# Two transformer blocks on one core: some transfers go to ScalarE's queue, the merges' operands become 66 wide, the order is planned anew

## Chip, cores, metric

One core of a Trainium2 chip. The metric is the device time of one execution in microseconds; the time before is the median of three runs.

## What is computed

Two blocks in a row on 256 tokens of width 1024, fp32 in and out. The first has block attention and differential attention with a table of relative biases, attention to a memory of 256 rows, and a gated feed-forward layer of 2816; the second an RWKV-7 layer with 12 heads of 64, memory attention and feed-forward, then a latent-attention layer with the same. What the change touches:

```python
logits = logits + bias_ht[h_i[..., None], rel_bucket(dist)]     # first block: biases by distance

def step(state, inp):                                           # second block: RWKV-7 scan over tokens
    r_t, w_t, k_t, v_t, a_t, b_t = inp
    sa = jnp.einsum('bhvk,bhk->bhv', state, a_t)
    state = (state * w_t[:, :, None, :] + sa[..., None] * b_t[:, :, None, :]
             + v_t[..., None] * k_t[:, :, None, :])
    return state, jnp.einsum('bhvk,bhk->bhv', state, r_t)
```

## The kernel before

**Matrix products.** Each fp32 product is three TensorE (PE) products of halves: a panel of weights (`wr`, 128 x 1024 numbers, 512 KB, three buffers) comes in by SP's queue, is cast to its high half `wh` on ScalarE (ACT) or VectorE (DVE), and DVE subtracts to get `wl`; activations are held as `ah` and `al`. The products gather in PSUM tiles `acc`; all other PSUM tiles are `pst`.

**The order.** The program is written as tasks (coroutines) whose operations are recorded first. The class `Order` then plans them: a list scheduler with a cost for each operation, a latency from engine to engine, times for DMA queues (`DMA_ISSUE`, `DMA_START`), a price for changing between widths of stationary operands (`turn`), and tables: `RUSH` moves the due times of a kind of task, `LEAN` and `SIDE` set what runs on which of two engines. What comes out is one fixed list for each engine, DMA issues included, since an issue stands in the queue of the engine that makes it. Each engine runs its list in order and waits where it must. The planner's costs decide the list, nothing at run time does. All recorded instructions are issued from one line, 2730 in the profile of before.

**Start.** `first_norm` loads the tokens `x` (`xres`) in four pieces; `load_gains` loads all gains; both stand in SP's queue between panels of `w_in`. ACT loads its function table, casts panels, and makes `ah` from x and gains.

**Bias table.** `rel_bias` makes a vector of biases (`relvec`) with three small matmuls, writes it to DRAM (`relonce`), writes it out 24 times (`rel`), and reads it back as the table `bias` in two transfers of 768 KB. DVE adds `bias` to the scores (`e`), ACT takes exponentials, and TensorE transposes them.

**The inverses.** The scan is done in two chunks of 128 tokens for 12 heads, 24 units, each with a unit triangular matrix of 128 x 128 to invert (`inverses`). `products` multiplies `bt` by `ar`, masks into `m271` (first chunk, halves `l` and `h`) and `m272` (second), and writes to DRAM (`d_m`). `substitute` reads the 32 x 32 blocks on the diagonal into rows (`kk` for the first chunk, a `tm` stage for the second) and substitutes in 31 steps of two instructions, the first chunk on POOL, the second on DVE; it writes the result to `d_x`. In `rwkv`, `expand` reads `d_x` into `xt` and DVE multiplies by a mask; `grams` makes the masked products `mk`, `mr` of two heads at a time; `merge` joins the blocks to 64 and to 128 for four units at a time, six times. Its matmuls have as stationary operands the inverse `xt`, the masked matrix (`mb(u)`) and zero-padded copies `y4`, `y2` in `ymerge`; 144 instructions of these are 64 columns wide:

```python
nc.tensor.matmul(p[:64, 1, i], y4[:, i], pairs(xt[:, u]), start=True, stop=True)
nc.tensor.matmul(p[:, i], self.mb(u)[:, 64:], x[:, i, :64], start=True, stop=True)
nc.tensor.matmul(p[:, i], y2[:, i], xt[:, u, 64:], start=True, stop=True)
```

Of the kernel before, what the change touches and what calls it, by code (L numbers as in the profile page):

```python
# [266 lines left out]
class Order:  # L267
# [22 lines left out]
    DMA_ISSUE = {"sync": 450.0, "gpsimd": 1000.0}  # L290
    DMA_START = {"sync": 1100.0, "gpsimd": 1900.0}
# [124 lines left out]
    def play(self, succs, preds, level, back):  # L416
# [9 lines left out]
        order, dma, table = [], 0.0, None  # L426
# [62 lines left out]
        while len(order) < len(ops):  # L489
            if events:  # L490
                i = events.pop()
                finish(i, ready[i] if back else 0.0)
                continue
            at, e = min((free[e] if here[e] else max(free[e], coming[e][0][0]), e) for e in names if here[e] or coming[e])
            while coming[e] and coming[e][0][0] <= at + self.EPS:
                i = heapq.heappop(coming[e])[1]
                heapq.heappush(here[e], (-level[i], i))
            i = heapq.heappop(here[e])[1]
            if not opened(i, at):
                continue  # L500
            op, start = ops[i], max(ready[i], free[e])
            if op.what != "dma_start":
                cost = op.cost
                if op.port:
                    start = max(start, port["gpsimd" if e == "vector" else "vector"])
                elif e == "tensor" and not back:
                    start = max(ready[i], free[e] + self.turn(mode, op.mode))
                    mode = op.mode
                    if start > free[e] + self.COLD:
                        slow = start + self.WARM  # L510
                    if start > free[e] + 40.0 and start == ready[i]:
                        cost += self.FILL
                    if start < slow:
                        cost *= 1.8
                end = start + cost
                if op.tables and table not in op.tables:
                    table = op.tables[0]
                    end += self.TABLE
                free[e] = end
                if op.port:  # L520
                    port[e] = end + self.PORT
            elif back:
                dma = max(dma, ready[i]) + op.size / 360.0
                free[e] = end = max(free[e] + self.DMA_ISSUE[e], dma + self.DMA_START[e])
            else:
                free[e] = start + self.DMA_ISSUE[e]
                dma = end = max(dma, start + self.DMA_START[e]) + op.size / (360.0 if start > self.DMA_COLD else 240.0)
            finish(i, end)
# [57 lines left out]

LEAN = {'ab0': 2895, 'carry': 137, 'diff_heads': 125, 'expand1': -3988, 'ffn': 1004, 'w_out': -297, 'gate': 3000, 'small': 4209, 'grams1': 1044, 'a_w_out': 168, 'mix_qk': -3000, 'grams0': 161, 'solve1': 808, 'merge1': 1298, 'a_r384': 3000, 'ab1': 6275, 'room': 128, 'mem': 1690, 'w_in': 770, 'cross_kv_w': 61, 'cross': -65, 'expand0': 537, 'down_w': -84, 'norm1': -235, 'a_lora2304': -49, 'rope': 3462, 'first': -431, 'a_mem_out': 1112, 'b_mem_heads': -246, 'a_mem_kv': -519}

SIDE = {'last': 'vector', 'gate': 'vector', 'kk': 'vector', 'rope': 'vector', 'sq': 'vector', 'x': 'vector'}

# [144 lines left out]
class Net(Sched):  # L737
# [1390 lines left out]
    def inverses(self, filler):  # L2128
# [36 lines left out]
        def substitute(c):  # L2165
# [16 lines left out]
            for i in range(2):  # L2182
                nc.sync.dma_start(ms[48 * i:48 * i + 48], d_m[c].strided(0, [[32 * 128 + 32, 48], [128, 32], [1, 32]]))
# [603 lines left out]
```

## Time and profile before

| | |
|---|---|
| runs | 1138.84, 1139.57, 1144.20 us; median 1139.57 |
| profiled execution | 1143.02 us, span 1141.3, mean granted TensorE clock 0.986 |
| busy share of the span | PE 97%, weight loads 92%, DVE 75%, ACT 38%, POOL 15% |
| TensorE products of the panels (`acc`) | 73% of the chain that ended last |
| transfers | 183.27 MB, 161 GB/s on the mean |

The span is from the first to the last instruction of the profiled execution; times in the rows below are from its start. An engine's idle time is put down to what ended it.

### The profile page before, as it was taken

Reading aid. Unit: us, or ns where it says so; the run is one execution under the profiler, and the core shown is the slowest. Engines: PE = TensorE matmul, PEld = TensorE weight load, DVE = VectorE, ACT = ScalarE, POOL = GpSimd, SP = SyncE. Lnnn points to the kernel's source line nnn. Section 1 sums busy time; section 2 is a strip of 40 time slices with the busy share of each in tenths; the row PEclk is TensorE's granted clock in tenths of the full one; section 3 lists DMA queues with packets and bytes.
Section 4 is the critical chain, followed back from the end, with each engine's and each line's share of the span. In section 5 each row is a group of like instructions: output and inputs, shape, how many; then the busy total and the mean of one; then the engine's idle time right before and its main releaser. Section 6 shows DMA issues by size and latency. Waiting matters only on the chain.

```text
span 1141.3 us, 21650 instructions
## 1 busy us (share of the span) xinstructions
PE 1110.4 (97%) x8716; PEld 1052.6 (92%) x8716; DVE 854.8 (75%) x1454; ACT 429.5 (38%) x857; POOL 171.3 (15%) x199
## 2 busy tenths in 40 slices
PE   8899999999999999899979999999999999999997
PEld 7798999999999999799768999999999889999985
DVE  7658577677776777979787877766878968777584
ACT  5437442545223214635323532223235765212400
POOL 1200101024111013016601121120012002111100
PEclk9999999999999999899989999999999999999999
DMA  8744355266564655347320355556654425555563
GB/s 260 231 153 145 120 176 181 86 193 208 168 208 140 214 187 180 121 117 215 102 65 14 96 182 180 176 163 186 195 169 140 153 95 170 184 185 179 175 207 105
DMA packets 116164, 183.27 MB, mean 161 GB/s; under 512 B 19175, under 2 KB 41480, under 8 KB 116040
## 3 DMA queue, kind: packets, MB, share of 16 engines
q1 hardware_dynamic: 115920, 181.37, 51.8%
q8 instruction: 68, 1.11, 0.4%
q0 software_dynamic: 144, 0.52, 0.2%
q14 instruction: 32, 0.26, 0.1%
HBM read 178.84 MB, written 3.48 MB: 160 GB/s over the span
## 4 chain that ended last, share of the span: by engine, by line
PE 84%; DVE 8%; DMA 4%; ACT 2%; issue 1%; SPq 0%; POOLq 0%; POOL 0%; ACTq 0%; DVEq 0%
PE acc L2730 73%; PE pst L2730 11%; DVE wl L2730 3%; DMA wr<-in_w_in_dram 1%; DVE e L2730 1%; ACT wh L2730 1%; DMA wr<-in_a_ffn_down_dram 1%; DVE tm L2730 1%; DVE qt L2730 0%; DMA wr<-in_b_w_out_dram 0%; DMA wr<-in_w_down_dram 0%; ACT e L2730 0%; DVE wh L2730 0%; DMA xres<-in_x_t_dram 0%; DMA wr<-in_a_ffn_gu_dram 0%
## 5 line engine op out<-in xcount | busy, mean ns | idle before, releaser
L2730 DVE TENSOR_TENSOR wl<-wr,wh 128x1024 fp32r<-128x1024 f32 (+3 forms) x358 | 411.4, 1157 | 107.5 <-ACT wh L2730 93.9
L2730 PE MATMUL acc<-ah,wh 128*128 128x256 f32 x2224 | 482.9, 283 | 4.6 <-ACT ah L2730 2.3
L2730 PE MATMUL acc<-ah,wl 128*128 128x256 f32 x2224 | 481.4, 284 | 2.0 <-DVE wl L2730 1.7
L2730 PE MATMUL acc<-al,wh 128*128 128x256 f32 x2224 | 481.6, 283 | 0.4 <-DVE al L2730 0.4
L2730 PEld LDWEIGHTS acc<-ah,wh 128*128 128x128 f32 x2224 | 357.9, 189 | 10.1 <-ACT ah L2730 3.6
L2730 PEld LDWEIGHTS acc<-ah,wl 128*128 128x128 f32 x2224 | 357.3, 189 | 5.7 <-DVE wl L2730 3.4
L2730 PEld LDWEIGHTS acc<-al,wh 128*128 128x128 f32 x2224 | 357.6, 189 | 2.7 <-DVE al L2730 1.3
L2730 ACT CAST wh<-wr 128x1024 fp32r<-128x1024 f32 (+4 forms) x199 | 181.3, 915 | 371.0 <-PE acc L2730 284.0
L2730 DVE CAST wh<-wr 128x1024 fp32r<-128x1024 f32 (+2 forms) x159 | 115.2, 726 | 68.1 <-PE acc L2730 46.8
L2730 POOL TENSOR_TENSOR h<-h,bc 128x512 f32<-128x512 f32 x33 | 51.6, 1568 | 267.9 <-ACT h L2730 267.7
L2730 PE MATMUL acc<-wh,ah 128*128 128x512 f32 (+2 forms) x212 | 66.2, 372 | 2.6 <-ACT wh L2730 2.4
L2730 PE MATMUL acc<-wl,ah 128*128 128x512 f32 (+2 forms) x212 | 66.1, 370 | 0.7 <-DVE wl L2730 0.5
L2730 PE MATMUL acc<-wh,al 128*128 128x512 f32 (+2 forms) x212 | 66.7, 373 | 0.0
L2730 POOL TENSOR_TENSOR tm<-tm 128x512 f32<-128x512 f32 (+1 forms) x18 | 27.4, 1525 | 222.3 <-ACT tm L2730 188.3
L2730 PEld LDWEIGHTS acc<-wh,ah 128*128 128x128 f32 x212 | 39.8, 193 | 9.4 <-ACT wh L2730 3.2
L2730 PEld LDWEIGHTS acc<-wl,ah 128*128 128x128 f32 x212 | 39.9, 192 | 7.9 <-DVE wl L2730 1.3
L2730 PEld LDWEIGHTS acc<-wh,al 128*128 128x128 f32 x212 | 39.8, 192 | 7.0 <-issue 0.3
L2730 ACT ACTIVATE h<-h 128x512 f32<-128x512 f32 x33 | 20.4, 629 | 62.3 <-DVE h L2730 62.1
L2730 ACT CAST ah<-h 128x512 fp32r<-128x512 f32 x32 | 19.7, 621 | 39.4 <-DVE h L2730 39.2
L2730 ACT ACTIVATE ah<-xres,gains 128x256 fp32r<-128x256 f32 x55 | 24.9, 500 | 16.4 <-DVE xres L2730 14.9
L2730 DVE TENSOR_TENSOR xres<-acc,xres 128x512 f32<-128x512 f32 x24 | 16.3, 687 | 18.9 <-PE acc L2730 18.8
L2730 DVE SCALAR_TENSOR_TENSOR al<-xres,gains,ah 128x256 fp32r<-128x256 f32 x56 | 28.6, 542 | 1.0 <-ACT ah L2730 0.9
(350 smaller groups left out, 1027.6 us busy)
## 6 DMA issues: line engine op xcount, KB each, us to landing
wr<-in_a_ffn_gu_dram SPq DMA_DIRECT2D x40, 512.0 KB, 3.8
wr<-in_b_ffn_gu_dram SPq DMA_DIRECT2D x40, 512.0 KB, 3.9
wr<-in_w_in_dram SPq DMA_DIRECT2D x22, 512.0 KB, 4.6
wr<-in_w_down_dram SPq DMA_DIRECT2D x22, 512.0 KB, 4.6
wr<-in_a_ffn_down_dram SPq DMA_DIRECT2D x22, 512.0 KB, 4.5
wr<-in_b_ffn_down_dram SPq DMA_DIRECT2D x22, 512.0 KB, 3.8
wr<-in_w_gate_dram SPq DMA_DIRECT2D x20, 512.0 KB, 4.3
wr<-in_w_up_dram SPq DMA_DIRECT2D x20, 512.0 KB, 4.0
```

Of the source, the lines that this page charges most:

```text
L2730: emit(*map(again, x.args), **{k: again(v) for k, v in x.kw.items()})
```

## The change

1. The planner gets a third DMA queue, that of ACT, and a transfer clock for each queue instead of one for all.
2. From SP to ACT go the issues of the gains, of x, of the bias chain (`rel_bias_table`, `rel_onehot`, `relonce`, `rel`, `bias`), and of the inverses (writes and reads of `d_m` and `d_x`, `sub_start`). Weights, memory and the rest stay on SP. x and gains are issued ahead of ACT's table load.
3. Three of the merge's stationary operands are 66 columns wide; the two more columns make two rows of output that nobody reads. `ymerge` is laid out flat so that the slice exists, and two columns behind the masked matrices are zeroed.
4. `SIDE`, `LEAN` (one value, `rope` 3462 to 4671) and all of `RUSH` have new values; the memory's tiles of the first block come from another pool, with two buffers for `mem_2`.

```diff
-    DMA_ISSUE = {"sync": 450.0, "gpsimd": 1000.0}
-    DMA_START = {"sync": 1100.0, "gpsimd": 1900.0}
+    DMA_ISSUE = {"sync": 450.0, "scalar": 450.0, "gpsimd": 1000.0}
+    DMA_START = {"sync": 1100.0, "scalar": 1100.0, "gpsimd": 1900.0}
...
-SIDE = {'last': 'vector', 'gate': 'vector', 'kk': 'vector', 'rope': 'vector', 'sq': 'vector', 'x': 'vector'}
+SIDE = {'gate': 'vector', 'kk': 'vector', 'rls': 'vector', 'rope': 'vector', 'x': 'vector', 'ms': 'vector', 'rk': 'vector'}
...
+        self.x = cp.tile([128, 8, S], F32, name="xres")
+        self.load_gains()
         nc.scalar.activation(self.small(1, "warm", 1), self.neghalf[:, :1], AF.Square)
...
-        self.nc.sync.dma_start(gt, self.a["gains"])
+        self.nc.scalar.dma_start(gt, self.a["gains"])
...
-            nc.sync.dma_start(bias[:, j:j + 128].rearrange("p j h -> p (j h)"),
+            nc.scalar.dma_start(bias[:, j:j + 128].rearrange("p j h -> p (j h)"),
...
-                nc.sync.dma_start(d_m[c][6 * i:6 * i + 6, :128].rearrange("u s t -> s u t"), self.mbs[c, i])
+                nc.scalar.dma_start(d_m[c][6 * i:6 * i + 6, :128].rearrange("u s t -> s u t"), self.mbs[c, i])
...
-            nc.sync.dma_start(last, self.d_x[c].rearrange("u b s t -> (b s) u t"))
+            nc.scalar.dma_start(last, self.d_x[c].rearrange("u b s t -> (b s) u t"))
...
-    def mb(self, u):
+    def mb(self, u, lo, hi=128):
         c, h = divmod(u, 12)
-        return self.mbs[c, h // 6][:, h % 6]
+        return self.mflat[c, h // 6][:, h % 6 * 128 + lo:h % 6 * 128 + hi]
...
+            wide = [[y[:, self.task.slot, i, 64 * j:64 * j + 66] for j in range(4)] for i in range(2)]
...
-                nc.tensor.matmul(p[:64, 1, i], y4[:, i], pairs(xt[:, u]), start=True, stop=True)
+                nc.tensor.matmul(p[:66, 1, i], wide[0][i], pairs(xt[:, u]), start=True, stop=True)
...
-                nc.tensor.matmul(p[:, i], self.mb(u)[:, 64:], x[:, i, :64], start=True, stop=True)
+                nc.tensor.matmul(p[:, i], self.mb(u, 64, 130), x[:, i, :64], start=True, stop=True)
...
-                nc.tensor.matmul(p[:, i], y2[:, i], xt[:, u, 64:], start=True, stop=True)
+                nc.tensor.matmul(p[:, i], wide[1][i], xt[:, u, 64:], start=True, stop=True)
```

How the lists move is shown at three places; a number behind a name is the tile's, and differs between the two programs.

The bias table. SP's list before, from the copy `rel` of the biases on:

```order
L2730 DMA wr_471<-in_w_in_dram 128x2x512
L2730 DMA rel<-relonce 24x4608
L2730 DMA wr_509<-in_w_ck_dram 128x2x512
L2730 DMA wr_522<-in_w_in_dram 128x2x512
L2730 DMA bias<-rel 128x1x1536 x2
L2730 DMA wr_559<-in_w_in_dram 128x2x512
L2730 DMA wr_591<-in_w_in_dram 128x2x512
```

ACT's list now, from the first transfer of the biases on, and TensorE's list now, from the last products ahead of the transposes of `e` on (`ka,qa`, the scores that `e` is made of, stand six products earlier than the first row, the products ahead of these count 15 in all):

```order
L2736 DMA relonce<-relvec 128x36
L2736 DMA rel<-relonce 24x4608
L2736 DMA bias<-rel 128x1x1536 x2
L2736 ACTIVATE memt_214<-memt_214 128x512
L2736 ACTIVATE memt_215<-memt_215 128x512
L2736 CAST wh_616<-wr_540 128x1024
L2736 ACTIVATE ah_87<-memt_577,gains 128x256 x2
L2736 CAST wh_648<-wr_569 128x1024
```

```order
L2736 MATMUL acc_0_650<-wl_589,ah_81 128x512
L2736 MATMUL acc_1_653<-wl_589,ah_81 128x512
L2736 MATMUL acc_0_650<-wh_566,al_82 128x512
L2736 MATMUL acc_1_653<-wh_566,al_82 128x512
L2736 MATMUL acc_0_650<-wh_566,ah_81 128x512
L2736 MATMUL acc_1_653<-wh_566,ah_81 128x512
L2736 MATMUL acc_0_650<-wl_589,ah_81 128x512
L2736 MATMUL pst_672<-ident,e_245 128x128 x3
L2736 MATMUL pst_677<-ident,e_246 128x128
```

The bias and the weight panels no longer share a queue; ACT's list has the transfers where SP had them, ahead of the cast `wh_616`. On TensorE the transposes of `e` stood before behind 48 products, now behind 15.

The normalization of the second block. TensorE's list before and now, around the transposes of `rstd`, whose result DVE uses to empty `acc`:

```order
L2730 MATMUL acc_1_5223<-al_5051,wh_5269 128x256
L2730 MATMUL acc_0_5230<-ah_5001,wl_5281 128x256
L2730 MATMUL acc_1_5223<-ah_5001,wl_5281 128x256
L2730 MATMUL pst_5357<-ident,rstd_5303 128x128 x2
L2730 MATMUL pst_5360<-ident,rstd_5315 128x128 x2
L2730 MATMUL acc_0_5373<-ah_4528,wh_5310 128x256
L2730 MATMUL acc_0_5373<-al_4545,wh_5310 128x256
L2730 MATMUL acc_0_5373<-ah_4528,wl_5322 128x256
```

```order
L2736 MATMUL acc_0_5241<-ah_4934,wl_5252 128x256
L2736 MATMUL acc_1_5249<-ah_4934,wl_5252 128x256
L2736 MATMUL pst_5331<-ident,rstd_5303 128x128 x2
L2736 MATMUL pst_5334<-ident,rstd_5316 128x128 x2
L2736 MATMUL acc_0_5241<-ah_4934,wh_5267 128x256
L2736 MATMUL acc_0_5241<-al_5049,wh_5267 128x256
L2736 MATMUL acc_0_5241<-ah_4934,wl_5283 128x256
L2736 MATMUL acc_0_5241<-ah_4934,wh_5267 128x256
L2736 MATMUL acc_0_5241<-al_5049,wh_5267 128x256
L2736 MATMUL acc_0_5241<-ah_4934,wl_5283 128x256
L2736 MATMUL acc_1_5249<-ah_4934,wh_5267 128x256
L2736 MATMUL acc_0_5241<-ah_4934,wh_5267 128x256
```

Before, the products behind the transposes begin a new pair of `acc` (5373), which DVE has to free first; now 18 products of the pair in progress stand there, the first eight of which are shown, and the new pair follows them.

The stretch before the first merge. DVE's list before and now, up to the mask on `xt`, which the transposes at the head of the first merge wait for (`tm` are the steps of the second chunk's substitution):

```order
L2730 TENSOR_TENSOR mr<-pst_6748,masks 128x128
L2730 TENSOR_TENSOR tm_6435<-tm_6421,tm_6435 96x133
L2730 TENSOR_TENSOR vtok<-vtok,vmean 128x256
L2730 TENSOR_TENSOR tm_6435<-tm_6435 96x7x19
L2730 TENSOR_TENSOR vtok<-vtok,bonus 128x256
L2730 TENSOR_TENSOR tm_6435<-tm_6421,tm_6435 96x126
L2730 TENSOR_TENSOR tm_6435<-tm_6435 96x7x18
L2730 TENSOR_TENSOR vtok<-vtok,vmean 128x256
L2730 TENSOR_TENSOR tm_6435<-tm_6421,tm_6435 96x136
L2730 TENSOR_TENSOR vtok<-vtok,bonus 128x256
L2730 TENSOR_TENSOR tm_6435<-tm_6435 96x8x17
L2730 TENSOR_TENSOR xt<-xt,m_6458 128x12x96
```

```order
L2736 TENSOR_TENSOR tm_6425<-tm_6425 96x7x18
L2736 TENSOR_TENSOR tm_6425<-tm_6446,tm_6425 96x136
L2736 TENSOR_TENSOR mk_6761<-pst_6747,masks 128x256
L2736 TENSOR_TENSOR tm_6425<-tm_6425 96x8x17
L2736 TENSOR_TENSOR mk_6761<-pst_6749,masks 128x256
L2736 TENSOR_TENSOR tm_6425<-tm_6446,tm_6425 96x128
L2736 TENSOR_TENSOR mr<-pst_6747,masks 128x128
L2736 TENSOR_TENSOR tm_6425<-tm_6425 96x8x16
L2736 TENSOR_TENSOR mr<-pst_6749,masks 128x128
L2736 TENSOR_TENSOR tm_6425<-tm_6446,tm_6425 96x135
L2736 TENSOR_TENSOR tm_6425<-tm_6425 96x9x15
L2736 TENSOR_TENSOR xt<-xt,m_6466 128x12x96
```

The mask on `xt` stands behind substitution steps in both; the `vtok` instructions that stood between them come after it now, and a set of `mk` and `mr` more stands ahead.

## Rows read from the trace of the kernel before

**Rows 1.** The page, part 4: the chain that ended last, by engine.
```profile
PE 84%; DVE 8%; DMA 4%; ACT 2%; issue 1%; SPq 0%; POOLq 0%; POOL 0%; ACTq 0%; DVEq 0%
```

**Rows 2.** TensorE's waits: what waited <- for what, us, times, longest.
```profile
PE pst L2730 <- DVE xt L2730: 4.2, 1, 4.2
PE acc L2730 <- ACT wh L2730: 2.8, 2, 2.4
...
PE acc L2730 <- DVE tm L2730: 1.8, 1, 1.8
...
PE pst L2730 <- DVE mr L2730: 1.3, 1, 1.3
PE pst L2730 <- ACT sq L2730: 1.2, 1, 1.2
```

**Rows 3.** Stretches: length, busy PE PEld DVE ACT POOL, granted clock, DMA share, GB/s.
```profile
20.00:40.00 20.00, 20.00 (x162) 19.32 (x162) 15.58 (x23) 3.28 (x6) 6.33 (x5) 1.00 0.92 248
40.00:48.60 8.60, 5.67 (x18) 3.94 (x17) 5.66 (x13) 5.78 (x13) 0.00 (x0) 0.82 0.63 213
583.20:588.40 5.20, 5.08 (x27) 4.67 (x28) 4.46 (x16) 1.43 (x3) 0.00 (x0) 0.52 0.01 3
```

**Rows 4.** Timeline of the start: start us, us, engine, line, instruction, idle before.
```profile
0.79 1.28 ACT L2730 ACT_TABLE_LOAD   x1 [0.79 <-PEq L2784]
...
5.19 0.62 ACT L2730 CAST wh<-wr 128x512 fp32r<-128x512 f32 x1 [0.41 <-DMA wr<-in_w_in_dram]
...
5.73 0.21 DVE L2730 TENSOR_SCALAR subg<-gains 128x1 f32<-128x1 f32 x2 [0.22 <-DMA gains<-in_gains_dram]
...
7.71 0.61 PE L2730 MATMUL acc<-ah,wh 128*128 128x256 f32 x2 [1.86 <-ACT ah L2730]
```

**Rows 5.** Timeline from 28 to 43 us, the bias table.
```profile
28.52 1.29 SPq L2730 DMA_DIRECT2D bias<-rel  x2
...
41.45 0.59 DVE L2730 CUSTOM_DVE_ANT_0 e<-pst,bias 128x256 f32<-128x256 f32 x1 [3.87 <-DMA bias<-rel]
```

**Rows 6.** The chain of waits from 456 to 464 us: start, us, what.
```profile
455.94 2.96 PE acc L2730 x25
...
458.93 0.84 ACT wh L2730
...
460.75 0.61 DVE tm L2730
...
461.40 2.11 PE acc L2730 x10
```

**Rows 7.** The chain of waits from 570 to 590 us.
```profile
569.98 2.46 PE pst L2730 x21
...
573.81 1.22 DVE wl L2730
...
577.04 0.33 DVE mk L2730
...
578.48 0.20 DVE mr L2730
...
581.38 1.27 DVE xt L2730
```

**Rows 8.** SP's queue from 575 to 577 us.
```profile
575.62 0.37 SPq L2730 DMA_DIRECT2D xt<-d_x  x1
```

**Rows 9.** TensorE's timeline at the merges, 588 to 606 us.
```profile
596.08 1.15 PE L2730 MATMUL pst<-xt,ymerge 128*64 128x64 f32 x16
597.15 0.43 PE L2730 MATMUL pst<-ry,xt 128*128 128x64 f32 x2
597.52 0.68 PE L2730 MATMUL pst<-x,m271l 128*64 128x64 f32 x8
598.12 0.88 PE L2730 MATMUL pst<-ry,xt 128*128 128x64 f32 x6
```

**Rows 10.** DMA issues from 505 to 605 us: KB each, us to landing.
```profile
d_m<-m272h SPq DMA_DIRECT2D x1, 384.0 KB, 6.3
```

More of the change, by code (lines that the diff above doesn't have):

```diff
@@ L425, in play @@
         events, ends = [], [0.0] * len(ops)
-        order, dma, table = [], 0.0, None
+        order, dma, table = [], dict.fromkeys(names, 0.0), None
         port, slow, mode = {"vector": 0.0, "gpsimd": 0.0}, 0.0, None
@@ L522, in play @@
             elif back:
[L523 to L524 removed]
+                dma[e] = max(dma[e], ready[i]) + op.size / 360.0
+                free[e] = end = max(free[e] + self.DMA_ISSUE[e], dma[e] + self.DMA_START[e])
             else:
                 free[e] = start + self.DMA_ISSUE[e]
[L527 removed]
+                end = max(dma[e], start + self.DMA_START[e]) + op.size / (360.0 if start > self.DMA_COLD else 240.0)
+                dma[e] = end
             finish(i, end)
@@ new lines @@
+LEAN = {'ab0': 2895, 'carry': 137, 'diff_heads': 125, 'expand1': -3988, 'ffn': 1004, 'w_out': -297, 'gate': 3000, 'small': 4209, 'grams1': 1044, 'a_w_out': 168, 'mix_qk': -3000, 'grams0': 161, 'solve1': 808, 'merge1': 1298, 'a_r384': 3000, 'ab1': 6275, 'room': 128, 'mem': 1690, 'w_in': 770, 'cross_kv_w': 61, 'cross': -65, 'expand0': 537, 'down_w': -84, 'norm1': -235, 'a_lora2304': -49, 'rope': 4671, 'first': -431, 'a_mem_out': 1112, 'b_mem_heads': -246, 'a_mem_kv': -519}
+SIDE = {'gate': 'vector', 'kk': 'vector', 'rls': 'vector', 'rope': 'vector', 'x': 'vector', 'ms': 'vector', 'rk': 'vector'}
@@ L782, in setup @@
             nc.tensor.matmul(self.pst(), zero[:, :128], zero, start=True, stop=True)
-        self.x = cp.tile([128, 8, S], F32, name="xres")
-        self.load_gains()
     def load_gains(self):
@@ L1516, in rel_bias @@
         once = self.dr.tile([128, 36], F32, name="relonce")
-        nc.sync.dma_start(once, vec)
+        nc.scalar.dma_start(once, vec)
         yield 0.0
         rows = self.dr.tile([m, n], F32, name="rel")
-        nc.sync.dma_start(rows, once.strided(0, [[0, m], [1, n]]))
+        nc.scalar.dma_start(rows, once.strided(0, [[0, m], [1, n]]))
         bias = pool.tile([128, 256, 12], F32, name="bias")
@@ L2273, in merge @@
             xg = xt[:, 4 * g:4 * g + 4]
-            y4, y2 = (y[:, self.task.slot, i] for i in range(2))
+            y4, y2 = (y[:, self.task.slot, i, :256].rearrange("p (u s) -> p u s", u=4) for i in range(2))
+            wide = [[y[:, self.task.slot, i, 64 * j:64 * j + 66] for j in range(4)] for i in range(2)]
             pairs = lambda ap: ap.rearrange("p (b i t) -> p b i t", b=2, i=2)[:, :, 1]
```

36 lines of the change are left out of this document (19 added, 17 removed).

## The prediction

> **What bounds the kernel now.** I read the chain that ended last first: TensorE (PE) is 84% of it [rows 1], so a microsecond is won only where TensorE stands still or runs at the lower clock. Next I read what its queue waited for [rows 2]: a handful of single waits, the longest 4.2 us for `xt`, and none that repeats. Then the stretches with their granted clock [rows 3]: after a standstill the clock stays low for a while. From 583.2 to 588.4 us it averages 0.52 of 2.4 GHz, that is the 1.2 GHz level, and 5.2 us of work there would have taken about 2.7: a stall of 4.2 us costs 2.5 us more behind it. So the question is which of these stalls the change takes away, which it leaves, and which it makes. The profiled execution took 1143.02 us (span 1141.3, 1.7 around it), 3.4 above the median of 1139.57; every term below is a difference read in the profiled execution, and I take the sum from the median.
>
> **1. The start: +0.5 us.** Before, ScalarE (ACT) loads its table at 0.79 us and casts each panel as it lands; the gains land at about 5.7, and TensorE's first product stands at 7.71, waiting for `ah`, which needs x [rows 4]. Now ACT issues x and gains itself from the first moment, but its queue is in order and the issue of `rel_onehot` stands behind the landing of the gains, that of the table behind a weight panel; only then come the table load (1.28 us) and the first cast (0.62) [rows 4]. If gains land 0.5 to 1 us earlier than 5.7, the first cast ends at about 7.1 to 7.7, where TensorE's first product is today; afterwards ACT has casts to make up. I take +0.5. Ends: -1 (x earlier, nothing to make up), +3 (landing no earlier, casts one behind another).
>
> **2. The bias queue at 28 to 45 us: -2.0.** SP issues the two halves of the bias table at 28.52, and behind them in the same queue the weight panels `wr_559`, `wr_591`. VectorE (DVE) waits for the bias until 41.45 [rows 5], TensorE then 2.4 us for the cast of a late panel [rows 2], and the clock of 40 to 48.6 averages 0.82 [rows 3], which is about 1.5 us lost (8.6 x 0.18). With the bias on ACT's queue the panels no longer stand behind it, so the 2.4 us for `wh` can go. But the order pieces ahead show what comes next: on TensorE the transposes of `e`, which need the bias, now stand 15 matmuls behind `ka,qa` instead of 48. Should the bias land at 41.4 as today, its scores (0.59 us for the first [rows 5]), the exponentials and then the transposes come about 2 us after TensorE is there. All of the stall and the clock would be -3.9; a bias 2 us later than today, sharing the transfer engines with weights, +2. I take -2.0, about the middle.
>
> The Trainium skill speaks against this part ("DMA: Bandwidth & Descriptors", Rules for kernel authors): spreading transfers over SP, ACT and GpSimd gives no bandwidth, since all run on the same 16 engines; it only saves issue time. The row from 20 to 40 us, with those engines 92% busy [rows 3], agrees that there is little to give; by the rule alone this term is 0 and the sum -4.2.
>
> **3. The normalization of block 2 at 459 to 461: -2.5.** TensorE ends 25 products at 458.9, transposes `rstd`, and has nothing else until ACT has cast a panel (0.84), copied, and DVE made `tm` at 460.75: 1.8 us idle [rows 2, 6]. The next 10 products take 2.11 us, against 2.96 for 25 before [rows 6]: 0.21 instead of 0.12 each, 0.9 lost to the clock. Now 18 products (2.1 us) stand between the transposes and that wait, and ACT's cast stands ahead of the transposes instead of behind them: what is left of the path, two copies and `tm` (0.61), fits under 2.1. Against it: the transposes come 16 products (1.9 us) earlier, closer behind the reductions, which may cost 0.3. So 1.8 + 0.9 - 0.3 = 2.4, say 2.5. Ends -2.8 and -1.5.
>
> **4. The key norms at 483: -0.7.** TensorE waits 1.2 us for the third `sq` [rows 2]. Now the second group stands behind 32 products and more and is covered, but the first has its three pairs in a row right behind ACT's squares. I expect about 0.5 of waiting there in place of 1.2; ends -3 (with the clock) and +1.
>
> **5. The inverses at 570 to 583: 0.** This is the largest wait (4.2 for `xt`, 1.3 for `mr`) [rows 2], and the one at which the moved transfers aim: SP issues the read of `xt` only at 575.62, behind a weight panel [rows 8], and ACT can issue it at once. But the chain says that the transfer is not what came last. From 573.8 to 583.2 it runs through DVE without a gap: one `wl` (1.22), `mk` at 0.33, `mr` at 0.20, between them the steps of the second substitution and `vtok`, and `xt` last, 1.27 [rows 7]. Data that land sooner do not overtake this list. In the new order (piece ahead) DVE has between a landmark, the mask product three sets ahead of `xt`, and `xt` itself: two `mk`, two `mr`, one `wl` and two substitution instructions more and four `vtok` fewer; with the steps taken as `mr` and `vtok` (128x256 like `mk`) as `mk` that is 0.66 + 0.4 + 1.22 + 0.4 - 1.32 = +1.4 us. TensorE has one set of four heads more to do meanwhile, 16 matmuls at 0.117 (21 take 2.46 [rows 7]), 1.9 us. The two nearly cancel: TensorE waits some 5 us as before, in more pieces. I take 0; ends +3 and, if DVE reaches the landmark earlier than I think, -8 (5.5 of waits and 2.5 of clock).
>
> **6. Operands of 66 columns: -1.5.** 144 matmuls of the merges hold 64 columns. Sixteen in a row take 1.07 us (596.08 to 597.15), eight take 0.60 (597.52 to 598.12) [rows 9]: 0.059 for each further one and 0.13 for a visit. With 8 or 16 at a visit there are about 15 visits, 2.0 us, if 66 columns do away with the whole of it; loading 2 columns more is a few ns each. The merges also wait for copies, which hides some: -1.5. Ends 0 and -2.
>
> **7. The rest: 0, at 4 either way.** The table of priorities is new as a whole, so every engine's order differs everywhere. DVE takes two products of `r` and some small ones from POOL and gives it the last ones; both have room on average. What small waits go or come elsewhere I can't name.
>
> Sum: +0.5 - 2.0 - 2.5 - 0.7 + 0 - 1.5 = -6.2, so **1133.4 us**. A measurement of this kernel can tell about 0.5% from no change (5.7 us); the forecast lies just beyond it.
>
> **Rivals.**
> *DVE lets go at `xt`.* The waits of step 5 go after all, because the new order has the second substitution in step with TensorE. For it: they are the largest item, and the product of the first half is issued some 30 rows earlier. Against it: the sums in step 5. Two thirds of -8 beside the rest: 1128.
>
> *Bandwidth is the bound of the first 45 us.* Then step 2 gives nothing and casts stay late: 1135.4, with step 1 at +2 it is 1137. For it: 92% [rows 3]. Against it: the panels did wait behind the bias in one queue.
>
> *ACT is held by its transfers (slower).* Place: the reads `kk<-d_m` and `tm<-d_m` on ACT, which wait for the landing of `d_m`, 6.3 us after issue [rows 10]. Between the write and the read of the second half ACT has only about 1.5 us of other work; casts and copies out of PSUM stand behind. On SP the same wait held only weights that were ahead of need. Price: 4.8 us at each of two places if TensorE runs out of work that needs no ACT, and 2.5 for the clock once: -6.2 + 9.6 + 2.5 = +5.9, 1145.5. It decides from the point where TensorE has less than 4.8 us of such work; in the new order I count 57 matmuls between the two, which at 0.117 us each, and twice that where the trace shows two instructions for one of the program's, are 7 to 13 us, so it should hold.
>
> *The width changes nothing.* If the eight take 0.60 us as before, step 6 is 0: 1134.9; inside the forecast.
>
> **Chances.** The forecast, with 1130 to 1137 of its own, 0.42; DVE lets go 0.20; bandwidth 0.21; ACT held 0.17. The forecast splits at 1133.9: 0.28 faster, 0.14 the same; bandwidth gives 0.02 and 0.19. So 0.50 faster, 0.33 the same, 0.17 slower. The range leaves out the outer parts of the last and of the best case: 1123 to 1143.
>
> **What would show it.** Right: no wait for `tm` by the block 2 transposes and full clock there; eight 66-wide in under 0.5 us; TensorE still waiting for DVE ahead of `xt` while the transfer has long landed; a first product near 8 us. Wrong: waits of TensorE for ACT right behind 515 or 545 us (ACT held); a wait for `e` above 2 us near 41; an `xt` wait under 1 us.

## The result, and the profile after

The changed kernel takes 1148.57 us (median of five runs, 1147.21 to 1149.64) against 1139.57 (median of five, 1138.84 to 1144.20). The medians lie 9.0 us apart; the ratio, which is taken over all the runs and is used from here on, is 1.0066, 95% interval 1.0052 to 1.0081, so some 7.5 us slower. The forecast was 1133.4 in a range of 1123 to 1143; the time lies outside it, and it moved the other way. The profiled execution took 1147.45 us (span 1145.7), 4.4 more than that of before, which was one of the longer ones; so the two traces have 4.4 us to explain, and not 7.5.

The chain that ended last has lost four points of TensorE [rows 1] to ACT, DVE and issues (page, part 4):

```profile
PE 80%; DVE 9%; DMA 4%; ACT 3%; issue 2%; POOL 0%; ACTq 0%; POOLq 0%; DVEq 0%
```

TensorE's waits answer to [rows 2]. The columns are again us in all, times, longest.

```profile
PE pst L2736 <- DVE ka L2736: 6.2, 1, 6.2
PE acc L2736 <- ACT wh L2736: 3.9, 4, 2.8
...
PE pst L2736 <- DVE mr L2736: 2.3, 2, 2.1
PE pst L2736 <- ACT vmean L2736: 2.2, 1, 2.2
...
PE pst L2736 <- DVE xt L2736: 1.0, 2, 0.8
```

The old largest wait, 4.2 us for `xt`, is down to 1.0; those for `tm` and `sq` are gone; `ka` with 6.2 and `wh` with 2.8 have come. To weigh them together with the clock I read the same six stretches of both kernels. What is lost in one is its length less PE's busy time, plus PE's busy time times (1 - granted clock). First the kernel before, columns as in [rows 3]:

```profile
0.00:20.00 20.00, 16.60 (x88) 13.29 (x89) 12.94 (x31) 13.53 (x26) 3.05 (x10) 0.91 0.81 269
20.00:60.00 40.00, 37.07 (x249) 33.33 (x249) 28.00 (x41) 14.20 (x26) 8.27 (x7) 0.96 0.78 227
60.00:120.00 60.00, 59.52 (x456) 54.92 (x456) 41.89 (x112) 32.24 (x86) 0.90 (x2) 1.00 0.44 136
440.00:500.00 60.00, 57.00 (x422) 53.56 (x421) 47.60 (x102) 31.05 (x68) 7.91 (x5) 0.91 0.40 121
500.00:560.00 60.00, 58.47 (x501) 53.26 (x501) 51.27 (x95) 26.36 (x64) 32.98 (x62) 1.00 0.66 179
560.00:640.00 80.00, 73.02 (x664) 65.02 (x663) 63.44 (x208) 25.06 (x67) 9.14 (x18) 0.94 0.14 34
```

and the changed kernel:

```profile
0.00:20.00 20.00, 15.29 (x70) 12.05 (x71) 10.25 (x22) 11.94 (x23) 1.19 (x9) 0.83 0.78 249
20.00:60.00 40.00, 33.44 (x227) 30.10 (x226) 29.15 (x57) 12.27 (x31) 6.54 (x8) 0.91 0.67 191
60.00:120.00 60.00, 57.62 (x439) 52.97 (x438) 42.88 (x107) 25.15 (x70) 2.43 (x2) 1.00 0.44 136
440.00:500.00 60.00, 59.17 (x474) 55.79 (x473) 51.00 (x103) 30.48 (x70) 16.82 (x18) 1.00 0.47 140
500.00:560.00 60.00, 56.40 (x453) 51.88 (x451) 51.89 (x87) 30.50 (x63) 26.16 (x53) 0.94 0.62 172
560.00:640.00 80.00, 74.90 (x683) 66.61 (x683) 64.31 (x215) 24.97 (x70) 9.39 (x20) 0.94 0.20 44
```

| us | lost before | lost after | difference | in slices of 2 us | forecast for it |
|---|---|---|---|---|---|
| 0 to 20 (start) | 4.9 | 7.3 | +2.4 | +2.5 | +0.5 (step 1) |
| 20 to 60 (bias) | 4.4 | 9.6 | +5.2 | +3.6 | -2.0 (step 2) |
| 60 to 120 | 0.5 | 2.4 | +1.9 | +1.9 | step 7 |
| 440 to 500 (normalization, key norms) | 8.1 | 0.8 | -7.3 | -6.8 | -3.2 (steps 3, 4) |
| 500 to 560 | 1.5 | 7.0 | +5.5 | +5.4 | step 7 |
| 560 to 640 (inverses, merges) | 11.4 | 9.6 | -1.8 | +0.2 | 0 (step 5) |

The mean clock of a long stretch also counts the time in which TensorE stands still, so a standstill at the lower clock is counted twice. The same reading in slices of 2 us avoids this and is the better one for 20 to 60 and for 560 to 640. The sum is +5.9, in slices +6.7; the wider operands, which make PE's busy time shorter and so don't show here, take 1.8 off it (below). That leaves 4.1 to 4.9, against 4.4. The loss stands in the first 120 us and between 500 and 560.

One profile is one execution, and four of the kernels below show how far a stretch varies by itself, since they run the same program up to 440 us: the kernel before, the one with only the inverses on ACT, and two with moves in block 2. In slices of 2 us they lose 5.1, 2.2, 2.6 and 5.3 us from 0 to 20, and 4.6, 5.0, 4.2 and 4.7 from 20 to 60. The changed kernel and two others with its start and bias on ACT lose 7.6, 6.0 and 5.9 from 0 to 20, and 8.1, 9.2 and 9.6 from 20 to 60. So both stretches do lose, the second more surely than the first.

The chain of waits from 0 to 50 us says how (start, us, what):

```profile
1.31 4.45 DMA gains<-in_gains_dram
5.78 0.57 ACTq L2736
...
6.82 1.28 ACT L2736
...
8.31 0.52 ACT wh L2736
...
30.34 12.29 DMA wr<-in_w_in_dram
...
42.72 0.69 DVE wh L2736
...
45.49 0.60 DVE ka L2736
...
46.14 1.65 PE pst L2736 x8
```

At the start ACT's queue stands at the issue of `onehot` until the gains have landed at 5.76, and only behind it come the table load and the first cast. TensorE's first product stands at 8.87 instead of 7.71 [rows 4], and the clock is up only at 15 us (granted 0.50 from 10 to 15 us, 0.99 from 15 to 20; before, 0.86 and 1.00). At 30 us a panel takes 12.29 us from issue to landing. The two queues of that moment (timeline, SP and ACT):

```profile
28.83 1.28 ACTq L2736 DMA_DIRECT2D bias<-rel  x2
30.34 3.04 SPq L2736 DMA_DIRECT2D wr<-in_w_in_dram  x2
```

The bias, 1.5 MB, is on ACT's queue, and the panel behind it in time on SP's queue; the median landing of a panel of `w_in` in this run is 4.5 us. That alone is no loss, for the panel that stood behind the bias in SP's own queue took as long, and landed at 42.39, where the changed kernel's landed at 42.63 (chain of waits of the kernel before):

```profile
29.91 12.48 DMA wr<-in_w_in_dram
```

What is new is what waits for the panel. Before, DVE copied `ka` at 36.30, ACT cast the panel at 42.47, and TensorE, which had its products with `ka` behind it, waited 2.4 us for that cast [rows 2]. DVE's new order has the panel's cast ahead of the copy of `ka`, so `ka` waits for the landing too, and TensorE stands still from 40.0 to 46.1.

### The profile page after: what moved, and what is told of

The parts are those of the page before. It is cut to its first block, busy times and chain, and to the rows that moved or that the text cites. A ratio compares the mean times of both kernels' runs of the same rounds, so it can differ in the third digit from the quotient of the medians.

```text
span 1145.7 us, 21647 instructions
## 1 busy us (share of the span) xinstructions
PE 1110.1 (97%) x8716; PEld 1053.3 (92%) x8716; DVE 862.9 (75%) x1473; ACT 423.9 (37%) x848; POOL 163.2 (14%) x193
## 4 chain that ended last, share of the span: by engine, by line
PE 80%; DVE 9%; DMA 4%; ACT 3%; issue 2%; POOL 0%; ACTq 0%; POOLq 0%; DVEq 0%
PE acc L2736 70%; PE pst L2736 11%; DVE wl L2736 3%; DMA wr<-in_w_in_dram 2%; ACT wh L2736 1%; DVE e L2736 1%; DVE wh L2736 1%; ACT e L2736 1%; DMA wr<-in_a_w_out_dram 1%; DMA wr<-in_b_ffn_down_dram 0%; DMA wr<-in_w_ck_dram 0%; DMA gains<-in_gains_dram 0%; DVE vtok L2736 0%; DVE kt L2736 0%; DVE al L2736 0%
## 5 line engine op out<-in xcount | busy, mean ns | idle before, releaser
L2736 ACT CAST wh<-wr 128x1024 fp32r<-128x1024 f32 (+3 forms) x193 | 174.8, 911 | 315.6 <-PE acc L2736 255.9
L2736 DVE CAST wh<-wr 128x1024 fp32r<-128x1024 f32 (+2 forms) x165 | 119.6, 727 | 73.1 <-PE acc L2736 44.5
L2736 POOL TENSOR_TENSOR rstd<-rms,neghalf 128x4 f32<-128x4 f32 (+2 forms) x11 | 12.9, 1178 | 147.4 <-DVE rms L2736 147.4
L2736 ACT ACTIVATE ah<-xres,gains 128x256 fp32r<-128x256 f32 x55 | 25.0, 499 | 11.4 <-DVE xres L2736 11.0
```

The costliest lines, as they stand in the source:

```text
L2736: emit(*map(again, x.args), **{k: again(v) for k, v in x.kw.items()})
```

## Experiments

Theory at the outset: the loss is in the first 60 us and comes from the queue of ACT, at the start and at the bias. First rival: the newly planned order loses, whatever the queue. Second: ACT is held at the inverses' transfers. Most kernels keep one of the two planned orders, word for word, and only change the engine that issues some transfers, just before the program is written out. `group` goes by the tile that is written: `start` is x, gains, `onehot`, `reltab`; `bias` is `relonce`, `rel`, `bias`; `inverses` is `d_m`, `sub_start`, `d_x`, `xt`. Ratios are to the kernel before, timed on the same chip, with 95% intervals; 0.1% is 1.14 us.

### The changed kernel with groups put back on SP

```diff
+    for op in ops:
+        if op.what == "dma_start" and group(op) in ('bias',):
+            op.engine = "sync"
```

The same with `('start',)`, with both, and with `('inverses',)`.

> The changed kernel with its planned order, but relonce, rel and the two halves of the bias are issued by SP again, at the same places of the order. Theory (the bias transfers on a queue of their own share the transfer engines with the weight panels, so that the panel which DVE casts ahead of the copy of ka lands late): TensorE's wait for ka of 6.2 us shrinks below 2, the clock of 40 to 60 us rises from 0.83 to over 0.9, and the time falls by 5 to 7 us, to 1142 to 1144. Rival (the newly planned order makes the stall, whatever the queue): the wait for ka stays above 4 us and the time within 2 us of 1148.6.

> The changed kernel, but x, gains, onehot and reltab are issued by SP again, at the same places of the order. Theory (ACT's first cast stands behind its own issues, which wait for the landing of gains and onehot): ACT loads its table in the first microsecond, the first product with a weight comes at 8 us or earlier instead of 8.9, full clock is reached at 11 instead of 15 us, and the time falls by 2 to 4 us, to 1145 to 1147. Rival (the first product waits for data, and the queue they come by is of no account): first product at 8.5 to 9.2 and a time within 1 us of 1148.6.

> Both moves back at once: x, gains, onehot, reltab, relonce, rel and bias on SP, the inverses' transfers stay on ACT, 66 columns. Theory: the two gains add up, 7 to 11 us, 1138 to 1142, so near the kernel before or below it by the 5 us which block 2 gained between 440 and 640 us. Rival (planned order): 1146 to 1149.

> The changed kernel, but the transfers of the inverses (d_m, sub_start, d_x, xt) are issued by SP at the same places of the order. Theory (on ACT they do not hold up anything that matters, on SP they stand among weight panels whose issue they delay): 0 to 5 us slower than the changed kernel, 1148.5 to 1153. Rival (ACT is held at the reads of d_m and that is the new wait of 2.2 us for vmean at 540 to 545): 2 to 4 us faster, 1145 to 1147, and the wait for vmean gone.

| back on SP | median us | ratio |
|---|---|---|
| bias | 1146.19 | 1.0057 (1.0042 to 1.0071) |
| start | 1144.97 | 1.0042 (1.0027 to 1.0058) |
| start and bias | 1142.02 | 1.0026 (1.0013 to 1.0039) |
| inverses | 1147.38 | 1.0070 (1.0053 to 1.0086) |

The start gives 0.24% back (2.7 us), as expected. The bias gives 0.09% where 0.4 to 0.6 were expected, no more than the intervals leave open, though the wait does shrink. TensorE's wait for `ka` with the bias on SP, and with the start alone on SP:

```profile
PE pst L2754 <- DVE ka L2754: 3.3, 1, 3.3
```

```profile
PE pst L2754 <- DVE ka L2754: 8.5, 1, 8.5
```

(8.5 because TensorE comes there earlier while the panel does not.) With both back, 0.40% are regained (4.6 us, where 7 to 11 were expected), and the kernel is still 0.26% slower than before: the rival has a share too. The inverses change nothing on either queue: the second rival is out for this order.

### One part at a time: width, order alone, queue alone

```diff
+            if x.what == "matmul" and x.args[1].shape[-1] == 66:
+                x.args = (x.args[0][:64], x.args[1][:, :64]) + tuple(x.args[2:])
```

> The changed kernel with its queues and its planned order, word for word, but the 144 stationary operands of the merges that are 66 columns wide are issued 64 wide again. Theory (as the forecast had it, a visit to the narrow operands costs TensorE 0.13 us): runs of eight in a row take 0.60 us instead of what they take 66 wide, and the time rises by 1 to 2 us, to 1149.5 to 1150.5. Rival (the width changes nothing): the same time within 0.7 us, the same busy time of TensorE from 585 to 640 us.

> The changed kernel's planned order and 66 columns, but every transfer issued by SP: the new order alone, without a queue of ACT. Theory (start and bias on ACT's queue are what lose; the inverses' transfers on ACT neither win nor lose): as with start and bias back, 1142 within 1.5 us. Rival (ACT's queue pays at the inverses): 1144 to 1146, with a wait for xt over 2 us.

> The kernel before, its planned order and 64 columns, but x, gains, onehot, reltab, the bias chain and the inverses' transfers issued by ACT: the queue alone, without the new order. Theory (the queue is what loses, at the start by table load and casts behind issues, at the bias by sharing): 1142 to 1147, 3 to 8 slower than before. Rival (the new order is what loses, the queue is free or pays): 1136 to 1140.

> The kernel before with only relonce, rel and the two halves of the bias issued by ACT. Theory (the ring of the bias takes packets away from the weight panels): 0 to 4 us slower, 1139 to 1143, a wait for a panel's cast or for ka of 3 us or more between 36 and 46 us. Rival (step 2 of the forecast: panels no longer stand behind the bias in one queue): 2 us faster, 1137, and the wait of 2.4 us at 43.6 gone.

| kernel | median us | ratio |
|---|---|---|
| changed, operands 64 wide | 1149.38 | 1.0077 (1.0054 to 1.0100) |
| changed order, every transfer on SP | 1142.17 | 1.0019 (1.0004 to 1.0033) |
| old order, all three groups on ACT | 1147.65 | 1.0062 (1.0044 to 1.0081) |
| old order, only the bias on ACT | 1142.01 | 1.0008 (0.9994 to 1.0023) |

The queue alone loses 0.62%, the order alone 0.19% (with the wide operands and the other places of the memory's tiles, which are part of that kernel); together they make 0.66. The difference from their sum, 0.81, is within the intervals. The bias on ACT costs the old order nothing that can be told, and gains nothing: in its profile a panel's cast is waited for 3.6 us there, against 2.4 [rows 2], and the panel that is issued just behind the bias, now on the other queue, takes 14.50 us to land instead of 12.48 (chain of waits of that kernel):

```profile
29.46 14.50 DMA wr<-in_w_in_dram
```

The time can't show the width (0.11% apart, intervals overlap), but the trace can, since both kernels have the same order and the same tiles and differ in nothing but the width of these instructions. TensorE's timeline in the merges, 64 wide:

```profile
619.95 0.68 PE L2740 MATMUL pst<-xt,ymerge 128*64 128x64 f32 x8
620.56 0.41 PE L2740 MATMUL pst<-x,m272h 128*96 128x96 f32 x2
...
624.53 0.80 PE L2740 MATMUL pst<-xt,ymerge 128*64 128x64 f32 x10
625.26 0.38 PE L2740 MATMUL pst<-ymerge,xt 128*96 128x64 f32 x2
625.57 0.56 PE L2740 MATMUL pst<-xt,ymerge 128*64 128x64 f32 x6
626.06 0.55 PE L2740 MATMUL pst<-ymerge,xt 128*96 128x64 f32 x4
```

and 66 wide:

```profile
620.89 0.64 PE L2736 MATMUL pst<-xt,ymerge 128*66 128x64 f32 x8
621.37 0.36 PE L2736 MATMUL pst<-x,m272h 128*96 128x96 f32 x2
...
625.06 0.76 PE L2736 MATMUL pst<-xt,ymerge 128*66 128x64 f32 x10
625.66 0.33 PE L2736 MATMUL pst<-ymerge,xt 128*96 128x64 f32 x2
625.83 0.52 PE L2736 MATMUL pst<-xt,ymerge 128*66 128x64 f32 x6
626.19 0.50 PE L2736 MATMUL pst<-ymerge,xt 128*96 128x64 f32 x4
```

From start to start: eight 0.61 against 0.48, ten 0.73 against 0.60, six 0.49 against 0.36, and the two 96-wide ones between them 0.31 against 0.17. Each change costs 0.13 to 0.14 us, into narrow operands and out of them. From the first product with `ymerge` to the sixteen of `st,ar` behind the last merge, 39.70 us pass 64 wide (592.20 to 631.90) and 37.87 us 66 wide (593.61 to 631.48): 1.8 us. TensorE's busy time in it falls by 2.9 us (37.89 to 35.02), and its idle time rises by 1.0 (1.81 to 2.85). The Trainium skill ("TensorEngine Tiling (Array Packing)", Key Properties) says that a change of the array's tiling mode drains TensorE first; a price at each change agrees with that, while no run here shows that a 64-wide operand is such a mode.

### What loses at the start, and what the old order does at the inverses

The first kernel has only `onehot` and `reltab` back on SP; the second only the inverses on ACT in the old order; the third the old order with SP's first nine issues in the new sequence:

```diff
+    new = [x[0], wr[0], gains[0], wr[1], x[1], wr[2], x[2], wr[3]]
```

The fourth is the changed kernel with start and bias on SP and two operations of DVE moved (`late` is the cast and the low half of the panel that stand ahead of `ka`):

```diff
+    order = [i for i in order if i not in late]
+    at = order.index(ka[1]) + 1
+    order[at:at] = late
```

> The changed kernel, but onehot and reltab alone are issued by SP again; x and gains stay with ACT. Theory (ACT, in order, is held by its own issues: that of onehot waits until gains or x has landed, and only behind it come the table load and the first cast): of the 2.8 us that all four issues back on SP gave, some 1 to 2 come back; the table load ends at about 6.5 instead of 8.1 us, the first product stands at 7.3 to 8 us instead of 8.9, and the time is 1146.5 to 1147.5. Rival (the issues are of no account, x and gains land late on this queue): first product as late as before within 0.3 us, 1148.5.

> The kernel before, but only the inverses' transfers (d_m, sub_start, d_x, xt) are issued by ACT, at their places in its order. With all transfers on ACT that kernel lost 0.62%, with the bias alone 0.08%. Theory (the rest is the start, ACT is not held long at the inverses): 0 to 0.2% slower, 1139 to 1142. Rival (the third of the forecast, ACT held at the reads of d_m): 3 to 5 us slower, 1142.5 to 1145, with TensorE waiting for ACT (fe, fp) 2 us and more between 540 and 560 us and for xt longer than 4.2.

> The kernel before, with SP's first nine issues in the changed kernel's order (the first quarter of x, a panel, gains, a panel, x, a panel, x, ...), everything on SP and nothing else touched. Theory (at the start it is the order of the transfers that is worth something, not the queue): first product at 6.3 to 6.8 us instead of 7.7, full clock from there on, 2 to 3 us faster than before, 1136.5 to 1138. Rival (it falls into the next stall, where the bias is waited for, at 41 to 46 us): the same time within 1 us.

> The changed kernel with start and bias on SP and, in DVE's order, the two copies of ka put ahead of the cast and the low half of the panel that they stood behind (that panel lands behind a half of the bias). Theory (DVE, in order, carries the wait for a late panel over to ka, which TensorE needs first): the wait for ka of 3.2 us falls below 1, and the time by 2 to 4 us against 1142.0, to 1138 to 1140. Rival (the scores need the bias anyway, the wait moves to e or to the next panel): a wait of 2 us or more for e, wh or wl between 40 and 48 us instead and a time within 1 us of 1142.

| kernel | median us | ratio |
|---|---|---|
| changed, `onehot`, `reltab` on SP | 1144.09 | 1.0027 (1.0014 to 1.0039) |
| old order, inverses on ACT | 1144.88 | 1.0031 (1.0019 to 1.0044) |
| old order, x first on SP | 1144.14 | 1.0027 (1.0016 to 1.0039) |
| changed, start and bias on SP, `ka` first | 1143.35 | 1.0021 (1.0009 to 1.0034) |

Those two small transfers, 0.05 MB, make 0.39% (4.4 us), as much as all four of the start. Without them ACT's table load comes as soon as x is issued (timeline of that kernel, ACT and PE):

```profile
5.22 1.28 ACT L2754 ACT_TABLE_LOAD   x1 [5.22 <-DMA xres<-in_x_t_dram]
...
7.28 0.50 PE L2754 MATMUL acc<-ah,wh 128*128 128x256 f32 x2 [1.04 <-ACT wh L2754]
```

The first product is 1.6 us earlier than in the changed kernel. In the old order the inverses on ACT do cost, 3.5 us; by the stretches of its profile 500 to 560 loses 2.9 against 1.5 us and 560 to 640 14.2 against 11.4. TensorE's waits for ACT's `fe` and `fp` grow from 1.1 to 2.1 us, and that for `xt` from 4.2 to 4.6; this does not make up the whole. x first made the old order slower, against both hypotheses: ACT's order has three casts of panels ahead of `ah`, the second and third of these panels now land later (their casts start at 7.03 and 8.31 us), and the first product stands at 9.39 us. And with `ka` first its wait is gone, but in its place stands

```profile
PE pst L2765 <- ACT e L2765: 5.7, 1, 5.7
```

The rival was right here. ACT's cast of the next panel waits 7.6 us for its landing, until 40.58; DVE has that panel's low half ahead of `e`, and ACT that cast. Moving one copy ahead of one late panel only puts the next piece behind the next late panel; whether an order that moves them all would win, no run shows.

### Position or queue, the bias again, and fewer bytes

```diff
+    casts = [i for i in order if ops[i].engine == "scalar" and wrote(ops[i]).startswith("wh")]
+    order = [i for i in order if i not in late]
+    at = order.index(casts[3]) + 1
+    order[at:at] = late
```

Here `late` is `onehot` and `reltab`, still on ACT's queue. The second kernel has these and the bias on SP; the third is the old kernel with one load, not read before 280 us, put off.

> The changed kernel with every transfer on the queue it chose; only the issues of onehot and reltab stand later in ACT's order, behind its fourth cast of a panel instead of ahead of its first. Theory (what lost at the start is that ACT's casts stood behind two issues that wait for a landing, not the queue): as with those two on SP, 0.2 to 0.35% slower than before, 1143 to 1145. Rival (transfers from ACT's queue cost in themselves): 0.55 to 0.7% slower, as the changed kernel.

> The changed kernel with onehot, reltab and the bias chain on SP, x and gains on ACT. Theory (the start's loss is those two issues, and the bias chain on ACT costs another 0.1%): 0.1 to 0.25% slower than before, 1141 to 1143.5, and TensorE's wait for ka under 4 us. Rival (with the start mended the bias is free on ACT): as with onehot and reltab alone, 0.27%, and a wait for ka of 6 us.

> The kernel before, where one load is issued later by SP: the first quarter of the second mem (mem_2t, 128x2x256, first read by ACT only near 280 us) goes from 10.95 us to behind three panels that follow the bias. Theory (up to 45 us the transfers are the bound, so 262 KB less ahead of the bias and its panels are worth what they take, some 1 us, and a little clock): 1 to 2 us faster, with the waits for wh and wl at 43 us down to 2 or less. Rival (the wait is set by the order of bias and panels, not by bytes): the same within 0.5 us.

| kernel | median us | ratio |
|---|---|---|
| changed, `onehot`, `reltab` later on ACT | 1145.29 | 1.0041 (1.0028 to 1.0054) |
| changed, `onehot`, `reltab`, bias on SP | 1144.51 | 1.0035 (1.0025 to 1.0045) |
| old, one load put off | 1140.08 | 0.9997 (0.9985 to 1.0010) |

Later on the same queue gives 0.25% back of the 0.39, with the first product at 7.33 us: most of the start's price is the position in ACT's order. Whether the rest is the queue stays open, the intervals overlap. The bias on SP on top gives nothing: over three pairs it gave 0.09, 0.16 and -0.08%. The load put off looks good in the profile (20 to 60 us loses 1.6 us there instead of 4.4) and is worth nothing in time:

```profile
20.00:60.00 40.00, 38.38 (x273) 35.07 (x273) 29.73 (x44) 14.29 (x26) 9.43 (x7) 1.00 0.82 245
```

It was that one execution: a kernel further below has the same load put off, and its profile loses 5.2 us from 20 to 60 in slices of 2 us. The kernel before itself ran between 1136.3 and 1144.3 over all runs here.

### Are the gains in block 2 real?

The old kernel and its queues, with what the new plan did at 455 to 484 us copied by hand. The numbers are places in the recorded list of operations: the four transposes of `rstd`; ACT's copies `tm`, `bc` and DVE's `tm`; the third `k`.

```diff
+    move([4252, 4253, 4269, 4270], 4347)
+    move([4254, 4271, 4285], 4378)
+    move([4594], 4593)
```

The second has the load put off as well. The third moves the rest of the chain too, `kk`, `dal` and two products:

```diff
+    move([4316, 4318, 4317, 4319, 4355], 4285)
+    move([4354], 4428)
+    move([4397, 4398], 4396)
```

> The kernel before, all its queues kept, with three moves by hand that do in its order what the new plan did between 455 and 484 us: the four transposes of rstd stand 14 products earlier on TensorE, ACT copies tm and bc ahead of its next cast and DVE makes tm ahead of that panel's low half; and DVE makes the third k ahead of a panel's low half and cast instead of behind them. Theory (steps 3 and 4 of the forecast were right, and it is the order that they live on): no wait for tm at 461 and under 0.5 us for sq at 483, 2 to 5 us faster than before, 1135 to 1138. Rival (what is won there is waited for again at the next transfer or at 577 to 583): the waits gone and the time within 1 us of 1140.

> The same with the first quarter of the second mem loaded behind the bias's panels as well. Theory: 0 to 1 us faster than with the moves alone, 1134 to 1138, the fastest of all. Rival: as the moves alone, or no faster than before.

> As the kernel before with the three moves, and the rest of that chain moved with them: ACT makes kk ahead of its cast, DVE the second half of kk and its half of dal ahead of that panel's low half, of qp and of xres, and two more products stand ahead of the product with dal on TensorE. With the three moves alone the wait for tm of 1.84 us was gone and dal was waited for 2.54 instead of 0.58. Theory (the gain of step 3 is real if the chain behind tm is moved as well): the wait for dal below 0.8 us, full clock from 460 to 480, and 3 to 5 us faster than before, 1135 to 1137. Rival (it is waited for again at the next piece of the chain or at xt): 1138 to 1139, as with the three moves alone.

| kernel | median us | ratio |
|---|---|---|
| old, three moves | 1138.51 | 0.9991 (0.9977 to 1.0004) |
| old, three moves, load put off | 1139.53 | 0.9992 (0.9978 to 1.0006) |
| old, whole chain moved | 1136.73 | 0.9976 (0.9961 to 0.9992) |

With three moves `tm` and `sq` are no longer waited for, but the next piece is:

```profile
PE pst L2739 <- ACT dal L2739: 2.5, 1, 2.5
```

With the whole chain moved 0.29 us of that is left, and from 440 to 500 us 2.2 us are lost instead of 8.1, at full clock:

```profile
440.00:500.00 60.00, 57.83 (x457) 53.31 (x456) 51.49 (x108) 31.22 (x68) 7.93 (x5) 1.00 0.38 120
```

That is the one kernel here whose interval lies below the kernel before, by 2.7 us, and the only version that comes out ahead of both. It was the last of eighteen and its interval ends 0.08% short of no change, so with so many tried it is not certain.

## Why the prediction was wrong, step by step

**What bounds the kernel: right.** Waits of TensorE and the clock behind them are the account: the six stretches and the width add up to 4.1 to 4.9 us, against 4.4.

**Step 1, start (+0.5): the mechanism was right, the size wrong.** The step said that the issue of `onehot` stands behind the landing of the gains and the table load and casts behind that. So it is. But it let the gains land 0.5 to 1 us earlier, and in the chain above they land at 5.76, no earlier than before [rows 4]. The stretch lost 2.4 us more, near the step's upper end of 3; in time all four transfers are 0.24%, 2.7 us, and those two issues alone 0.39%, 4.4 us.

**Step 2, bias (-2.0): failed, with the wrong sign.** "With the bias on ACT's queue the panels no longer stand behind it" is true of the queue and false of the landing. The panel issued behind the bias took 12.48 us before, in the same queue, 12.29 in the changed kernel, and 14.50 in the old order with only the bias on ACT: a queue of its own did not let it past. So the gain was not there. The step's other end, "a bias 2 us later, sharing the transfer engines with weights, +2", had the sharing, but put it on the bias instead of on the panel, and the step overlooked that DVE's new order has that panel's cast ahead of `ka`: 6.2 us of waiting in place of 2.4. Nor is -2.0 "about the middle" of -3.9 and +2; that would be -1.0. The Trainium skill ("DMA: Bandwidth & Descriptors", Issuing engines are not separate DMA queues) says that transfers issued by different engines run on the same 16 engines and interleave; landings of 12.29 and 14.50 us from two queues, against 12.48 from one, agree. By its rule the step was 0, and for the queue that is what the runs give in time: 0.08% in the old order, and 0.09, 0.16 and -0.08% between pairs in the new one. The rest of what the stretch lost is the new order: with every transfer on SP it loses 7.9 us in slices of 2 us, against 4.6 in the kernel before.

**Steps 3 and 4 (-2.5, -0.7): right, and too small in the profile.** From 440 to 500 us 7.3 us less are lost; no wait for `tm` or `sq`, full clock. The step took the clock's share from ten products (0.9), and the profiled execution ran the whole stretch at 0.91. In time, with the moves alone and the chain moved up to `dal`, it is 2.7 us (0.9 to 4.4), beside the forecast's 3.2; the first three moves by themselves can't be told from no change.

**Step 5, inverses (0): right as a sum.** The wait for `xt` went, `mr` took 1.0 us of it back and the clock stayed low: 10.1 lost instead of 10.0 in slices of 2 us. It is DVE that comes last, as the chain said: its mask on `xt` starts at 587.21. In the changed kernel `xt` is issued at 578.65 and lands after 4.4 us, while TensorE comes to its transposes at 590; and back on SP these transfers cost the same (1.0070 and 1.0066).

**Step 6, 66 columns (-1.5): right.** 1.8 us in the trace. The number is partly luck. The price of 0.13 a visit was one of two: it is paid on the way in and on the way out. At 17 visits in the trace both would be 4.6 us; TensorE's busy time fell by 2.9, and 1.0 of that came back as waiting. So the step had half the price and nearly the right count, and the rest was hidden.

**Step 7, the rest (0, at 4 either way): failed, and in time the largest miss.** The step gave no reason for its 0 but that the waits could not be named. 60 to 120 us lost 1.9 more and 500 to 560 us 5.5 more, 7.4 together. Part of that is one execution (with all transfers on SP the second stretch lost 4.7 instead of 7.0), but the order alone costs 0.19% in time, 2.2 us, with the gain of steps 3, 4 and 6 already in it. By the forecast those were -4.7, so what step 7 put at 0 comes to some +6.9, beyond its own end of 4. A part of it is the wait for `ka`, which step 2 should have seen: it stands at 2.6 us even with every transfer on SP. A plan that is new as a whole is no zero.

**Rivals.** *DVE lets go at `xt`*: the wait fell under 1 us as that rival said, the time did not come. *Bandwidth is the bound*: closest in its mechanism, since step 2 did give nothing; it had 1137 and no loss, because it left out the new order and the start's size. *ACT is held by its transfers*: closest in its number (1145.5), by luck: the sign was right and the place wrong. ACT is held at the start, by issues that wait for a landing. At the reads of `d_m` its queue is taken for 1.3 us at 524 in the changed kernel and, with the wait for the landing, for 2.5 us at 558, not for 4.8, and the wait for `vmean` at 541 has another cause, a late panel of `a_w_out` (ACT's timeline):

```profile
541.39 1.05 ACT L2736 CAST wh<-wr 128x1024 fp32r<-128x1024 f32 x1 [2.05 <-DMA wr<-in_a_w_out_dram]
```

In the old order the inverses on ACT do cost 0.31%. *The width changes nothing*: no, by the trace.

**The account in time.** From the kernel before to the changed one, with each piece the difference of two ratios, good to some 0.2%: order +0.19, inverses on ACT +0.07, bias on ACT +0.16, start on ACT +0.24, in all 0.66%. Beside the forecast, in us and good to some 2 each: the order 2.2 instead of -4.7 (step 7, off by 6.9), the bias 1.8 instead of -2.0 (step 2, off by 3.8; by the other two pairs 1.0 and -0.9), the start 2.7 instead of 0.5 (step 1, off by 2.2), the inverses 0.8 instead of 0. What stays open is how the order's 0.19% divides between 20 to 120 and 500 to 560 us, and what makes the inverses cost in the old order.

## What to carry to other kernels

Before a transfer is given to a computing engine, look for the issues that must wait for a landing: whatever the engine does next waits with them, and two transfers of 0.05 MB ahead of the first cast cost 4 us. Don't count on a second queue to let a panel past a large transfer (12.5 us to landing in one queue, 12.3 and 14.5 in two). Look instead which engine, in order, has an operation on the late panel ahead of one that the bottleneck needs. When a stall is moved away, look for the next piece of its chain: here the wait came back there until the chain was moved as a whole. A single profile of a kernel that varies by 0.3% does not tell whether it was worth anything: time the move alone. And a plan that is new everywhere is not 0 in a forecast: plan it without the other changes and measure that first.

## What the runs showed of the hardware that was not expected

- Eight products between operands of 96 columns take 0.61 us at 64 columns and 0.48 at 66, and two 96-wide ones between narrow runs 0.31 against 0.17: leaving the narrow width costs as much as entering it.
- A panel of 512 KB that lands in 4.5 us on the median took 12.48 us behind a transfer of 1.5 MB in the same queue, and 12.29 and 14.50 with that transfer on another engine's queue.
- Executions of one kernel lie 0.3% to either side of the median (1136.3 to 1144.3 us for the kernel before), and four profiles with the same program up to 440 us lost 5.1, 2.2, 2.6 and 5.3 us in the first 20.
